# Layer 0's expert stage with one fixed stream of weights and rows read by number

## The chip, the cores and the metric

The kernel runs on one core of a Trainium2 chip. It computes a whole two-layer model in one launch. The metric is the device time of one launch in microseconds (us), as the median of several runs. The engines are named as in the profile: PE multiplies matrices (PEld is its load of the stationary operand), DVE and ACT work on vectors, POOL is GpSimd, SP issues most transfers.

## The reference, cut to what matters

Each of the two layers ends in a mixture of 16 experts. Every token takes its best group of four experts, and in it the best two:

```python
def hier_moe(h, wg, bg, we, be, w1, w3, w2):
    ...
    combine = jnp.sum(jax.nn.one_hot(eid, N_EXPERTS, dtype=F32) * wts[..., None], axis=1)
    out = jnp.zeros((T, D), F32)
    for e in range(N_EXPERTS):
        y = (jax.nn.silu(h @ w1[e]) * (h @ w3[e])) @ w2[e]
        out = out + combine[:, e:e + 1] * y
    return out.astype(h.dtype)
```

In layer 0, T is 512 (256 latent and 256 context tokens), D is 1024, and an expert is 512 wide. Its weights are 1024x512 twice and 512x1024, in 32 bits: 6.29 MB an expert. Behind the mixture, the tokens (`x`) get its output times a gate, and layer 1 begins with a norm and a projection.

## The kernel before, in words

The change lies in layer 0's expert stage, `experts` with `all0`. The router has put each expert's tokens into a list of at most 96 (`cap`). The 512 tokens stand as four tiles of 128 (`NT`), each split into two parts, `hhi` and `hlo`: PE multiplies in a form that keeps fewer bits, so a factor is taken as high part plus low part, and a product is three matmuls (high by high, high by low, low by high). `split` (line 220) makes the two parts: ACT copies the high one (`whi`, `XT`, `gT`), then DVE subtracts it (`wlo`).

**The lists.** Experts go in four groups of four, so one group's lists have 4 x 96 = 384 places (`N`). `lists(g)` writes a matrix of zeros and ones, `Pg`, which has a one where a token stands at a place: DVE writes all four tiles of group 0 (L609), and half of those of later groups, POOL the other half (L614). `gather(g, k)` multiplies a 128-column piece of the token tiles with `Pg`, in eight matmuls of 128x384 (`ga`), and splits the result into `XT`. Eight such pieces make a group's rows. `gather_next(e)` does two of the next group's eight beside each expert.

**An expert.** `start0` reads eight units of weights (512 KB each, a DMA that SP issues) into a ring of eight places (`slots`: four of them in the stage's own pool, four in another), splits each unit and does its six matmuls of 96x512 (`h`). Then SiLU on ACT, the product on DVE (`gg`, L652), four transposes on PE (`gT`), and in `finish0` four units of `w2`, again six matmuls each, into two banks `y`. ACT copies one half of `y` (L819), DVE the other (L820), and POOL stores the 96 rows to the table `yD` in device memory. `start0` is a generator: the loop over `e` begins expert e+1 before it finishes e. Apart from that order of the code and a few order tokens, a scheduler (Tile) places the instructions on the engines' queues.

**The combination.** Experts 0 to 13 leave their rows in `yD`. After expert 13's code, eight indirect reads on POOL bring each token's two rows into `rooms`. During expert 15, ACT scales one row (L790), DVE adds the other and multiplies with the gate `g2` (L791, L792), POOL adds the result to `x` (L793). The last two experts don't go through the table: their `y` is scaled and split by `weighted` (L763, L764), multiplied with transposed ones (`PT`) into `sc`, and added to `x` by `add_y` (L767, L768). Then layer 1's norm follows, `norm_T1` (L327 on): it loads the norm's weights and four modulation rows, makes `whi<-whi,xn` (L338), squares (L344), scales (L345, L352), transposes, and the first projection `pj` can start.

**Full lists.** A list that overflows is caught by `beyond` (L671 on): a loop on all engines, whose count `nexp` is read from memory. For the data here the count is zero, so the loop is only crossed. In layer 0 its code stands behind expert 12's, in layer 1 at the end.

Of the kernel before, what the change touches and what calls it, by code (L numbers as in the profile page):

```python
# [11 lines left out]
F32 = mybir.dt.float32  # L12
F32R = mybir.dt.float32r
# [8 lines left out]
P = 128  # L22
# [7 lines left out]
NCST = 1268  # L30
# [24 lines left out]
def host_consts():  # L55
# [16 lines left out]
    c[:, C_SMALL:C_SMALL + 16] = np.arange(16)  # L72
    c[:, C_SMALL + 16:C_SMALL + 32] = np.tril(np.ones((4, 4)), -1).ravel()
# [58 lines left out]
def tile_kernel(ctx: ExitStack, tc: tile.TileContext, I, out, stage=99, dbg=None):  # L132
# [293 lines left out]
    def moe(l, tiles, cap, ng, x1, pm, pn, hhi, hlo):  # L426
# [165 lines left out]
        def experts(pe, ysb, rest, spare=None):  # L592
# [5 lines left out]

            def lists(g):

                Pg = pe.tile([P, NT, N] if l == 0 else [P, NT, ng, 2, cap], F32R, tag="Pg", name="Pg")
                iota = cst[:, C_IOTA + 1:C_IOTA + 1 + cap]
                for a in range(NT):
                    if l == 1:
                        V.tensor_tensor(Pg[:, a], iota[:, None, None, :].to_broadcast([P, ng, 2, cap]),
                                        rk[:, a, g * ng:(g + 1) * ng, None, None].to_broadcast([P, ng, 2, cap]),
                                        op=ALU.is_equal)
                    elif g == 0 or a % 2:
                        V.tensor_tensor(Pg[:, a].rearrange("p (e c) -> p e c", e=ng),  # L609
                                        iota[:, None, :].to_broadcast([P, ng, cap]),  # L610
                                        rk[:, a, g * ng:(g + 1) * ng, None].to_broadcast([P, ng, cap]), op=ALU.is_equal)
                    else:
                        for e in range(ng):
                            G.tensor_scalar(Pg[:, a, e * cap:(e + 1) * cap], iota, rk[:, a, g * ng + e:g * ng + e + 1],  # L614
                                            None, op0=ALU.is_equal)
                XT = [pe.tile([P, 8, N], dt, tag=f"XT{i}", name="XT", bufs=2)
                      for i, dt in enumerate((F32R, F32R) if l == 0 else (F32,))]
                groups[g] = (Pg, XT)

            def gather(g, k):  # L620

                Pg, XT = groups[g]
                acc = ps("ga", "ga")
# [8 lines left out]

            def start0(e, es_, XT):

                hs = []
                for m in ("moe_w1", "moe_w3"):
                    acc = ps("h", "h")
                    hs.append(acc[0:cap, :])
                    for hh in range(4):
                        w = wload(I[m][l, e, hh * 256:(hh + 1) * 256, :], 2, 512)  # L640
                        whi, wlo = split_tiles()
                        split(w, whi, wlo)
                        for kk_ in range(2):
                            k = hh * 2 + kk_
                            mm(acc[0:cap, :], XT[0][:, k, es_], whi[:, kk_], start=(k == 0), stop=False)
                            mm(acc[0:cap, :], XT[0][:, k, es_], wlo[:, kk_], start=False, stop=False)
                            mm(acc[0:cap, :], XT[1][:, k, es_], whi[:, kk_], start=False, stop=(k == 7))
                        if hh < 3 or m == "moe_w1":
                            yield
                gg = pe.tile([P, 512], F32, tag="gg", name="gg", bufs=l + 1)  # L650
                act(gg[0:cap], hs[0], AF.Silu)
                V.tensor_tensor(gg[0:cap], gg[0:cap], hs[1], op=ALU.mult)  # L652
                yield gg

            def finish0(e, gg):
                acc = ps("gT", "gT")
                for f in range(4):
# [1139 lines left out]
```

## Time and profile before

| | us |
|---|---|
| median of 3 runs | 1466.31 (1465.74 to 1469.53) |
| the profiled execution, its own time | 1464.7 |
| its span in the trace | 1462.9 |
| PE busy over the span | 1282.3 (88%) |
| DVE busy | 810.3 (55%) |
| ACT busy | 601.8 (41%) |
| POOL busy | 239.9 (16%) |

The profile is of one execution. Its time is 1.6 us below the median. What lies around the span is 1.8 us. The shares of the whole span mix stages: the expert stage of layer 0, from about 535 to 913 us, is read from its own stretches below. "Granted clock" is the share of full speed that PE was given in a stretch; 1.00 is its upper level, 2.4 GHz.

### The profile page before, as it was taken

To read this page: it belongs to the slowest core of one execution; us is meant where nothing else is said; L and a number is where in the kernel's file an instruction comes from. 1 tells how busy PE (TensorE), PEld (TensorE's weight loads), DVE (VectorE), ACT (ScalarE), POOL (GpSimd) and SP (SyncE) were. 2 spreads that over 40 slices of the span, in tenths; PEclk is the share of its full clock that TensorE was granted. 3 is DMA by queue.
4 is the path that set the end of the run, shared out by engine and by line. 5 is a ranking of instruction groups with operands and counts; after the bars stand their busy time and mean duration, and the time that the engine had idled before them with its cause. 6 is when DMAs were issued, how large, how long until landed. Compare 5 with 4: busy or idle time off the path is not lost. (4 is left out here: it accounts for less than half of the span.)

```text
span 1462.9 us, 22162 instructions
## 1 busy us (share of the span) xinstructions
PE 1282.3 (88%) x8412; PEld 829.1 (57%) x8412; DVE 810.3 (55%) x1492; ACT 601.8 (41%) x1000; POOL 239.9 (16%) x245
## 2 busy tenths in 40 slices
PE   5999778888979968999999786789998799998975
PEld 1556556666646756777777553677665644433321
DVE  1336846777746665888888668963627520110003
ACT  2752422222224334777777564433637321211102
POOL 1005422424113203030110025420000100000000
PEclk9999889998999969999999998799998889999998
DMA  9687677766772544999999787562352579999654
GB/s 343 212 253 234 180 192 180 196 181 162 199 239 78 210 141 161 335 322 332 318 338 337 271 298 259 130 172 73 101 208 64 191 256 394 394 395 393 250 218 171
DMA packets 237859, 342.93 MB, mean 234 GB/s; under 512 B 95192, under 2 KB 125176, under 8 KB 237488
## 3 DMA queue, kind: packets, MB, share of 16 engines
q1 hardware_dynamic: 226240, 304.72, 62.6%
q0 software_dynamic: 8800, 28.42, 5.9%
q10 hardware_dynamic: 2704, 8.27, 1.6%
q8 instruction: 70, 1.15, 0.3%
q14 instruction: 45, 0.37, 0.1%
HBM read 320.57 MB, written 20.79 MB: 233 GB/s over the span
## 5 line engine op out<-in xcount | busy, mean ns | idle before, releaser
L220 DVE TENSOR_TENSOR wlo<-w,whi 128x1024 fp32r<-128x1024 f32 (+1 forms) x296 | 322.7, 1103 | 153.2 <-ACT whi L220 147.2
L220 ACT ACTIVATE whi<-w 128x1024 fp32r<-128x1024 f32 (+1 forms) x296 | 273.0, 932 | 236.2 <-DMA w<-in_ev_w_in_dram 69.5
L210 PE MATMUL h<-whi,XT 128*96 128x512 f32 x512 | 167.7, 401 | 12.2 <-issue 8.4
L210 PE MATMUL pj<-hh,whi 128*128 128x512 f32 x432 | 147.9, 424 | 0.3 <-ACT hh L220 0.3
L210 PE MATMUL h<-w,XT 128*64 128x512 f32 x512 | 138.5, 614 | 5.4 <-DMA w<-in_moe_w_dram 5.4
L210 PEld LDWEIGHTS h<-whi,XT 128*96 128x96 f32 x512 | 84.1, 164 | 50.5 <-issue 9.8
L210 PE MATMUL h<-wlo,XT 128*96 128x512 f32 x256 | 102.7, 401 | 6.0 <-DVE wlo L220 6.0
L210 PEld LDWEIGHTS pj<-hh,whi 128*128 128x128 f32 x432 | 82.1, 198 | 31.7 <-issue 9.8
L210 PE MATMUL pj<-hh,wlo 128*128 128x512 f32 x216 | 89.2, 415 | 3.3 <-DVE wlo L220 3.1
L210 PE MATMUL y<-whi,gT 128*96 128x512 f32 x256 | 87.4, 413 | 4.4 <-ACT gT L220 1.7
L210 PE MATMUL ada<-w,sT 128*32 128x512 f32 x384 | 69.6, 652 | 16.0 <-DMA w<-in_ada_w_dram 9.4
L210 PEld LDWEIGHTS h<-w,XT 128*64 128x64 f32 x512 | 36.6, 138 | 64.0 <-issue 56.9
L764 DVE SCALAR_TENSOR_TENSOR ylo<-y,sw,yhi 128x512 fp32r<-128x512 f32 x16 | 12.0, 751 | 100.9 <-ACT yhi L763 100.9
L210 PE MATMUL y<-w,gT 128*64 128x512 f32 x256 | 64.7, 614 | 1.5 <-ACT gT L697 1.5
L688 DVE TENSOR_TENSOR gg<-gg,h 64x512 f32<-64x512 f32 x16 | 11.1, 692 | 95.0 <-ACT gg L687 95.0
L210 PE MATMUL ga<-Pg,hh 128*128 128x384 f32 x256 | 58.5, 358 | 4.7 <-POOL Pg L614 3.5
L210 PEld LDWEIGHTS y<-whi,gT 128*96 128x96 f32 x256 | 41.8, 167 | 27.4 <-DVE gT L220 5.3
L210 PEld LDWEIGHTS h<-wlo,XT 128*96 128x96 f32 x256 | 42.2, 165 | 25.0 <-DVE wlo L220 8.8
L210 PE MATMUL y<-wlo,gT 128*96 128x512 f32 x128 | 51.9, 405 | 3.7 <-DVE wlo L220 3.7
L210 PEld LDWEIGHTS ga<-Pg,hh 128*128 128x128 f32 x256 | 47.6, 199 | 10.7 <-POOL Pg L614 3.9
L210 PEld LDWEIGHTS pj<-hh,wlo 128*128 128x128 f32 x216 | 42.8, 198 | 18.0 <-DVE wlo L220 5.9
L1769 POOL TENSOR_TENSOR x<-x,fg 128x512 f32<-128x512 f32 x2 | 2.8, 1378 | 283.8 <-ACT sq L1768 283.8
(534 smaller groups left out, 2309.6 us busy)
## 6 DMA issues: line engine op xcount, KB each, us to landing
w<-in_moe_w_dram SPq DMA_DIRECT2D x384, 512.0 KB, 6.5
w<-in_ada_w_dram SPq DMA_DIRECT2D x96, 512.0 KB, 5.2
w<-in_ev_w_in_dram SPq DMA_DIRECT2D x27, 512.0 KB, 5.8
w<-in_od_w_in_dram SPq DMA_DIRECT2D x24, 512.0 KB, 4.6
yD<-ysb POOLq DMA_DIRECT2D x14, 384.0 KB, 6.3
sD<-wad SPq DMA_DIRECT2D x16, 256.0 KB, 3.1
w<-in_ev_w_out_dram SPq DMA_DIRECT2D x8, 512.0 KB, 4.4
w<-in_od_w_out_dram SPq DMA_DIRECT2D x8, 512.0 KB, 4.2
```

The source lines that it names most:

```text
L210: inst = nc.tensor.matmul(*args, **kw)
L220: for inst in (act(hi, src, AF.Copy), V.tensor_tensor(lo, src, hi.bitcast(F32), op=ALU.subtract)):
L688: V.tensor_tensor(gg[64:128], gg[64:128], acc[64:128], op=ALU.mult)
L764: V.scalar_tensor_tensor(lo, y, w, hi.bitcast(F32), op0=ALU.mult, op1=ALU.subtract))
L1769: (V if h else G).tensor_tensor(xt_[:, hs], xt_[:, hs], fg[:, hs], op=ALU.mult)
```

## The change

1. The lists of group 0 are gathered as before. The row order on PE is written out: gathers of four pieces, a unit of weights, two pieces, a unit, two pieces.
2. For groups 1 to 3 there are no gathers. `one_hot0` writes `Pg` (all on DVE), `ids` multiplies it with the tokens' numbers (a new constant, `C_TOK`) in 16 matmuls of one column, `fetch(e)` reads the expert's 96 rows of the normed tokens from device memory (`hD`) with one indirect DMA on POOL, `turn_rows` transposes them (8 transposes an expert) and splits them into `XE`.
3. Weights go as one `stream` of units; `weights(e, u)` has units split up to three ahead of their use. Eight more places of 512 KB are added to the ring, and taken out again behind expert 10.
4. PE, ACT and DVE follow the order in which the code is written, by order tokens ("line" for PE, "moe" for ACT and DVE).
5. Both halves of `y` are copied by ACT.
6. The rooms' sums go between expert 15's later units, as before in effect; reading them is issued at the end of expert 13's step.
7. `beyond` stands behind the last `add_y`.

The core of the diff:

```diff
+            def ids(g, Pg, put):
+                acc = ps("sw", "ga")
+                idt[g] = pe.tile([P, ng], I32, tag="idt", name="idt", bufs=2)
+                for i in range(ng):
+                    for a in range(NT):
+                        mm(acc[r, i:i + 1], Pg[:, a, i * cap:(i + 1) * cap], cst[:, C_TOK + a:C_TOK + a + 1],
+                           start=(a == 0), stop=(a == NT - 1))
+                put(V.tensor_copy(idt[g][r], acc[r, 0:ng]))
+            def fetch(e):
+                if ng <= e < 16:
+                    g, i = divmod(e, ng)
+                    xe[e] = pe.tile([P, D], F32, tag="xe", name="xe", bufs=2)
+                    nc.gpsimd.indirect_dma_start(
+                        out=xe[e][0:cap, :], out_offset=None, in_=hD,
+                        in_offset=bass.IndirectOffsetOnAxis(ap=idt[g][0:cap, i:i + 1], axis=0))
+            def turn_rows(e, h):
...
+                acc = ps("xt", ("ga", "ps")[h])
+                for k in range(4):
+                    flip(acc[:, k * cap:(k + 1) * cap], xe[e][0:cap, (4 * h + k) * 128:(4 * h + k + 1) * 128],
+                         ident[0:cap, 0:cap])
+                split(acc[:, 0:4 * cap].rearrange("p (k c) -> p k c", k=4), XTe[e][0][:, 4 * h:4 * h + 4],
+                      XTe[e][1][:, 4 * h:4 * h + 4])
...
+                slots.extend([(pP, t, 1, h) for t in ("kT", "y", "kkn") for h in range(2)] +
+                             [(cp, "x3", 1, h) for h in range(2)])
...
+                stream = [(0, u) for u in range(8)]
+                for e in range(15):
+                    stream += [(e + 1, 0), (e + 1, 1)] + [(e, u) for u in range(8, 12)] + [(e + 1, u) for u in range(2, 8)]
+                stream += [(15, u) for u in range(8, 12)]
...
+                def weights(e, u):
+                    ready(place[e, u] + 3)
+                    return there.pop((e, u))
...
+                in_line[0] = True
+                token[0] = "moe"
+                put = lambda inst: inorder(inst, "moe")
+                for k in range(4):
+                    gather(0, k, ("ga", "gT")[k % 2])
+                hidden(0, 0)
...
                     if e < 14:
                         o = ysb[:, e % 2, :]
-                        act(o[r, 0:512], y[0], AF.Copy)
-                        V.tensor_copy(o[r, 512:1024], y[1])
+                        for h in range(2):
+                            put(act(o[r, h * 512:(h + 1) * 512], y[h][r], AF.Copy))
                         nc.gpsimd.dma_start(yD[e * cap:(e + 1) * cap, :], o[r, :])
...
-                    gather_next(e)
-                    if e == 12:
...
-                        beyond(rooms)
...
+                    turn_rows(e + 2, 0)
+                    hidden(e + 1, 3)
+                    turn_rows(e + 2, 1)
+                    if j == 0 and g + 1 < NG:
+                        one = one_hot0((g + 1) * ng, ng, F32, put)
...
+                    for u in range(4, 8):
+                        hidden(e + 1, u)
+                        if u == 4 and j == 0 and g + 1 < NG:
+                            ids(g + 1, one, put)
...
                         add_y(t, hs_, acc, ysb[:, a % 2, hs_])
+                beyond(rooms)
+                warm(AF.Sqrt, rooms[0])
```

Line numbers of the changed kernel are 2 higher in front of the expert stage (L212 for L210, L222 for L220).

PE at the start of the stage. `ga` are the gathers, `h` the products with the first units of weights. Before:

```order
L210 MATMUL ga<-Pg,hh 128x384 x8
L210 MATMUL h<-whi,XT 96x512
L210 MATMUL h<-wlo,XT 96x512
L210 MATMUL ga<-Pg,hh 128x384 x8
L210 MATMUL h<-whi,XT 96x512 x2
L210 MATMUL h<-wlo,XT 96x512
L210 MATMUL ga<-Pg,hh 128x384 x8
```

And after:

```order
L212 MATMUL ga<-Pg,hh 128x384 x32
L212 MATMUL h<-whi,XT 96x512
L212 MATMUL h<-wlo,XT 96x512
L212 MATMUL h<-whi,XT 96x512 x2
L212 MATMUL h<-wlo,XT 96x512
L212 MATMUL h<-whi,XT 96x512
L212 MATMUL ga<-Pg,hh 128x384 x16
```

The gathers stand in blocks of 32 and 16, and a unit's six products are whole between them.

PE inside an expert, before, where gathers (`ga`) for the next group stand among the transposes and products:

```order
L210 MATMUL h<-whi,XT 96x512
L210 MATMUL ga<-Pg,hh 128x384 x2
L215 MATMUL gT<-cst,gg 128x96 x4
L210 MATMUL ga<-Pg,hh 128x384 x5
L210 MATMUL y_6423<-whi,gT 96x512
```

After, in the same place of a later expert, `xt` are the transposes of the rows read by number:

```order
L212 MATMUL y<-whi,gT 96x512 x2
L212 MATMUL h<-whi,XE 96x512
L212 MATMUL h<-wlo,XE 96x512
L212 MATMUL h<-whi,XE 96x512 x2
L212 MATMUL h<-wlo,XE 96x512
L212 MATMUL h<-whi,XE 96x512
L217 MATMUL xt<-cst,xe 128x96 x4
L212 MATMUL h<-whi,XE 96x512
```

Sixteen gathers an expert are gone, and eight transposes have come, in two blocks of four around a unit.

DVE where the stage ends, before; L338 and L345 to L347 are layer 1's norm:

```order
L764 SCALAR_TENSOR_TENSOR spare<-y_8862,sw,spare 96x512
L767 TENSOR_TENSOR ysb<-sc,g2t 128x512 x2
L338 SCALAR_TENSOR_TENSOR whi<-whi,xn 128x1024 x2
L768 TENSOR_TENSOR x_4758<-ysb,x_4758 128x512 x2
L767 TENSOR_TENSOR ysb<-sc,g2t 128x512 x2
L345 TENSOR_TENSOR xn<-x_4758,whi 128x512
L346 TENSOR_TENSOR st<-st 128x1
L768 TENSOR_TENSOR x_4758<-ysb,x_4758 128x512
```

And after, the last sums with what follows them; the rows from `nexp` on are the loop's:

```order
L764 TENSOR_TENSOR ysb<-sc,g2t 128x512 x2
L765 TENSOR_TENSOR x_4757<-ysb,x_4757 128x512 x2
L222 TENSOR_TENSOR wlo<-w,whi 128x512
L678 TENSOR_LOAD nexp
L679 COMPARE_AND_BRANCH
L679 UNCONDITIONAL_BRANCH x2
L1892 BRANCH_PREFETCH_HINT
```

The other twelve sums stand ahead of these in the same pairs. All sixteen are now ahead of the loop's branch, and every instruction of layer 1's norm behind it.

## Rows read from the trace of the kernel before

**Rows 1.** Stretches of 20 us, then one of layer 1: busy us by engine, granted clock, DMA

```profile
core 0: us, PE busy (x) PEld busy (x) DVE busy (x) ACT busy (x) POOL busy (x), PEclk, DMA share, GB/s
...
740.00:760.00 20.00, 20.00 (x92) 14.52 (x92) 16.86 (x17) 14.71 (x17) 0.55 (x1) 1.00 0.97 348
...
860.00:880.00 20.00, 16.83 (x74) 11.12 (x73) 16.35 (x16) 14.92 (x17) 11.02 (x9) 1.00 1.00 378
...
1210.00:1250.00 40.00, 40.00 (x193) 18.27 (x194) 3.80 (x6) 6.96 (x15) 0.00 (x0) 1.00 1.04 394
```

**Rows 2.** Timeline, start and length: ACT first reads y of experts 0, 11, 14, 15

```profile
581.49 0.58 ACT L819 ACTIVATE ysb<-y 96x512 f32<-96x512 f32 x1
...
805.42 0.58 ACT L819 ACTIVATE ysb<-y 96x512 f32<-96x512 f32 x1
...
877.69 1.24 ACT L763 ACTIVATE spare<-y,sw 96x512 fp32r<-96x512 f32 x2
...
911.83 1.38 ACT L763 ACTIVATE spare<-y,sw 96x512 fp32r<-96x512 f32 x2 [3.19 <-PE y L210]
```

**Rows 3.** Timeline of PE, from expert 11's last gather to expert 12's transposes

```profile
805.41 1.49 PEld L210 LDWEIGHTS ga<-Pg,hh 128*128 128x128 f32 x8
...
817.88 1.58 PEld L210 LDWEIGHTS sw<-comb,Pg 128*96 128x96 f32 x16
...
819.41 0.53 PE L215 MATMUL gT<-cst,gg 96*128 96x96 f32 x4
```

**Rows 4.** Lines by form, 580 to 820 us: busy, mean ns | idle before it

```profile
L220 DVE TENSOR_TENSOR wlo<-w,whi 128x1024 fp32r<-128x1024 f32 x143 | 173.8, 1224 | 30.3 <-ACT whi L220 28.8
...
L220 DVE TENSOR_TENSOR XT<-ga,XT 128x384 fp32r<-128x384 f32 x23 | 12.7, 553 | 5.7 <-ACT XT L220 5.7
...
L652 DVE TENSOR_TENSOR gg<-gg,h 96x512 f32<-96x512 f32 x12 | 8.1, 676 | 0.0
...
L609 DVE TENSOR_TENSOR Pg<-cst,rk 128x384 fp32r<-128x384 f32 x4 | 2.3, 576 | 0.0
```

**Rows 5.** Timeline of PE at the start: gathers of list 0, wait for list 1

```profile
540.65 2.77 PE L210 MATMUL ga<-Pg,hh 128*128 128x384 f32 x8
...
571.53 1.14 PEld L210 LDWEIGHTS ga<-Pg,hh 128*128 128x128 f32 x4 [3.95 <-POOL Pg L614]
```

**Rows 6.** DMA issues, 530 to 940 us: count, KB, median us to landing

```profile
yD<-ysb POOLq DMA_DIRECT2D x14, 384.0 KB, 6.3
...
wlo<-adaD POOLq DMA_DIRECT2D x2, 512.0 KB, 4.2
...
room<-yD,idx POOLq DMA_INDIRECT x8, 8.9
```

**Rows 7.** Lines by form, 876 to 913 us

```profile
L220 DVE TENSOR_TENSOR wlo<-w,whi 128x1024 fp32r<-128x1024 f32 x12 | 18.9, 1605 | 2.5 <-ACT whi L220 2.5
...
L793 POOL TENSOR_TENSOR x<-room,x 128x1024 f32<-128x1024 f32 x4 | 13.5, 3364 | 9.7 <-DVE room L792 9.7
```

**Rows 8.** Timeline at the full lists' loop, layer 0, then layer 1

```profile
831.59 1.23 DVE L220 TENSOR_TENSOR wlo<-w,whi 128x1024 fp32r<-128x1024 f32 x1 [0.15 <-ACT whi L220]
...
838.89 0.74 PE L210 MATMUL h<-whi,XT 128*96 128x512 f32 x1 [8.42 <-issue]
...
1403.02 0.69 DVE L688 TENSOR_TENSOR gg<-gg,h 64x512 f32<-64x512 f32 x1 [7.22 <-ACT gg L687]
...
1404.61 1.30 SPq L701 DMA_DIRECT2D w<-in_moe_w_dram  x3
```

**Rows 9.** Timeline from layer 0's last expert to layer 1's first projection

```profile
912.54 1.45 DVE L764 SCALAR_TENSOR_TENSOR spare<-y,sw,spare 96x512 fp32r<-96x512 f32 x2 [2.65 <-ACT spare L763]
...
918.91 1.29 DVE L768 TENSOR_TENSOR x<-ysb,x 128x512 f32<-128x512 f32 x2
...
919.63 0.63 ACT L344 ACTIVATE xn<-x 128x512 f32<-128x512 f32 x1 [3.87 <-DVE x L768]
...
935.05 0.79 PE L210 MATMUL pj<-rT,whi 128*128 128x256 f32 x2
```

More of the change, by code (lines that the diff above doesn't have):

```diff
@@ L631, in gather @@
                     act(XT[0][:, k], acc[:, 0:N], AF.Copy)
[L633 to L653, printed above, removed]
@@ L705, in finish1 @@
                 return y
-            start, finish = ((start0, finish0), (start1, finish1))[l]
             def beyond(room):
@@ L775, in all0, with without @@
                 nc.gpsimd.dma_start(yD[Z:Z + P, :], zt)
-                rooms = []
                 order = [(2, 2), (3, 3), (0, 0), (1, 1)]
                 r = slice(0, cap)
-                steps = begin(0)
+                base = list(slots)
+                slots.extend([(pP, t, 1, h) for t in ("kT", "y", "kkn") for h in range(2)] +
+                             [(cp, "x3", 1, h) for h in range(2)])
+                turn[0] = 0
+                def without(tags):
+                    n = len(slots)
+                    slots[:] = [s_ for s_ in (slots[(turn[0] + i) % n] for i in range(n)) if s_[1] not in tags]
+                    turn[0] = 0
@@ new lines, in weights, with hidden @@
+                def weights(e, u):
+                    ready(place[e, u] + 3)
+                    return there.pop((e, u))
+                hs = {}
+                def hidden(e, u):
+                    X, es_ = (XTe[e], r) if e in XTe else (groups[0][1], slice(e * cap, (e + 1) * cap))
+                    whi, wlo = weights(e, u)
+                    if u % 4 == 0:
+                        hs[e, u // 4] = ps("h", "h")[r, :]
+                    acc = hs[e, u // 4]
+                    for i in range(2):
+                        k = u % 4 * 2 + i
+                        mm(acc, X[0][:, k, es_], whi[:, i], start=(k == 0), stop=False)
+                        mm(acc, X[0][:, k, es_], wlo[:, i], start=False, stop=False)
+                        mm(acc, X[1][:, k, es_], whi[:, i], start=False, stop=(k == 7))
@@ new lines, in all0 @@
+                    for f in range(4):
+                        flip(acc[:, f * cap:(f + 1) * cap], gg[r, f * 128:(f + 1) * 128], ident[r, 0:cap])
+                    gT = [pe.tile([P, 4, cap], F32R, tag=f"gT{i}", name="gT", bufs=2) for i in range(2)]
+                    split(acc[:, 0:4 * cap].rearrange("p (f c) -> p f c", f=4), *gT)
+                    if e < 15:
+                        hidden(e + 1, 1)
+                    y = [ps("y", "y") for _ in range(2)]
+                    for f in range(4):
+                        whi, wlo = weights(e, 8 + f)
+                        for i, (gh, w) in enumerate(((gT[0], whi), (gT[0], wlo), (gT[1], whi))):
+                            for h in range(2):
+                                mm(y[h][r], gh[:, f, :], w[:, h], start=(f == 0 and i == 0), stop=(f == 3 and i == 2))
```

206 lines of the change are left out of this document (117 added, 89 removed).

## The prediction

> **What bounds the kernel now.** I read the 20 us stretches first, then the dated rows of one engine, then the lines by form for the price of a row. In a steady stretch of layer 0's experts PE is busy 20.00 of 20 us at granted clock 1.00, DVE 16.86, ACT 14.71, and the transfers run at 348 GB/s with a share of 0.97 [rows 1]. So PE's own work ends last, with transfers close behind. That the transfers can do more is seen twice in the same group: 378 GB/s between 860 and 880 us, 394 in layer 1.
>
> The stage is dated by the moment at which ACT first reads an expert's `y` [rows 2]. Expert 0 is at 581.49, expert 11 at 805.42: 223.93 / 11 = 20.36 us per expert. Expert 14 is at 877.69, so experts 0 to 14 take 296.2, and expert 15 takes 34.1 more (911.83). The 14 periods at 20.36 would be 285.0; the other 11 us are around the loop and expert 13's extra work.
>
> What is PE's 20.36 made of? Between the end of the gathers at 805.41 + 1.49 = 806.90 and the next foreign row at 817.88 [rows 3] stand 48 products of 512 columns with no gap: 10.98 / 48 = 0.229 each. An expert has 72: 16.47 us. Its four transposes take 0.53 (0.132 each). Sixteen gathers at 1.49 / 8 = 0.186 take 2.98. Sum 19.98, so 0.38 of a period is waiting.
>
> **The change, part by part.** The sum is made against the profiled execution, 1464.7 us, which is 1.6 below the median of the runs.
>
> *Gathers out, rows by number in.* PE loses 2.98 per expert and gains eight transposes, 8 x 0.132 = 1.06, for experts 4 to 15. From the first `y` of expert 0 to that of expert 14 PE now has 14 x (16.47 + 0.53) = 238.0; transposes of 12 experts, 12.7; the numbers of three groups, 16 one-column products each, for which the 16 loads of `sw` in 1.58 us [rows 3] are the like: 4.7; the ones of experts 14 and 15, eight transposes and as many small products, 2.6 at most. Sum 258.0. That is the floor.
>
> *Waiting on top.* DVE per expert: 12 `wlo` at 1.224, `gg` 0.676, the low part of `gT` and two of `XE`, 128x384 each like `XT`, at 0.553, together 17.0; and in each group four `Pg` at 0.576 [rows 4], 0.6 per expert. Copying half of `y` goes to ACT, which had 5.3 us of 20 free. So DVE has 17.6 us to do in a PE period of 18.06, while its order is now fixed and weights may be split only three units ahead. I take 0.7 us of waiting per expert, about twice the 0.38 of now, and 1 us for each of the three bursts of `Pg` (2.3 us on DVE in one piece, partly under split units): 12.8. So experts 0 to 14 take 258.0 + 12.8 = 270.8 where they took 296.2: **25.4 won**. Ends: no waiting beyond the present rate wins 33 (14 x 0.38 = 5.3); at the present period of 20.36 only the loop's detour is won, some 11. The plain expert is then 18.75 us.
>
> *Places and transfers.* Per expert 12 x 524 KB, 393 KB of rows read and 393 KB stored to `yD`: 7.08 MB, in 18.75 us 378 GB/s, where it is 6.68 MB in 20.36 now, 328 GB/s. The 14 periods need 99.1 MB. Eight more places let 4.2 MB be there before expert 0 is through, since nothing but free places holds them back; the remaining 94.9 MB in 270.8 us is 350 GB/s, as in the steady row [rows 1]. I therefore cost transfers at nothing, with little to spare: if the lead is lost, the rival below takes over. One row read on POOL is of the size of a room's read, 8.9 us to landing [rows 6], and is asked for over one period ahead of its transposes: nothing.
>
> *The start.* PE now does 8 x 4 gathers at once, without waiting for units in between, and no longer stands 3.95 us for lists that POOL writes [rows 5]. Behind that wait it ran at half clock, as at 540.65, where eight gathers took 2.77 instead of 1.49. The two are worth at most 3.95 + some 5. Against it, the first products wait for the last piece's split and for unit 0 behind it. I take 5 of 0 to 9.
>
> *Expert 15.* The four sums of rooms on ACT, DVE and POOL stay; DVE's `wlo` took 1.605 instead of 1.224 there, and POOL's adds 3.364 each [rows 7]. PE loses nothing but waits. Without the transfers queued behind the loop I take 1.4 won, 8 either way.
>
> *The loop to the end.* At layer 0's loop DVE's last row ended at 832.82 and PE went on at 838.89, 6.1 us; at layer 1's, with no transfers in flight, SP went on 0.9 us behind DVE's end [rows 8]. At its new place little is in flight: I take 2.5 of 0.9 to 6.1. Dearer is what it parts. Now, the sums begin at 912.54, the norm's squares at 919.63 among them, and the projection starts at 935.05 [rows 9]: 22.5 us. After it, all 16 additions and multiplications at 0.645 (1.29 for two) must end first: 10.3, and 2.1 in front of them for `weighted` and the first `sc`: 12.4. Then the loop, 2.5. Then the norm from its start: 919.63 to 935.05 is 15.4 as it stands, with additions in between that fall away; but the load of the norm's weights (512 KB, like `wlo<-adaD`, 4.2 us [rows 6]) stands behind the loop now, and products wait for it. I take 18 of 15 to 22. Sum 32.9 for 22.5: **10.4 lost**, 6 to 18.
>
> *Sum.* 25.4 + 5 + 1.4 - 10.4 = 21.4 won: 1443.3 for the profiled execution, 1445 for the median.
>
> **The rivals.**
>
> *Transfers bound.* If the lead isn't made or doesn't last, the 99.1 MB go at the steady row's 348 GB/s: 284.8 us for 270.8, and 14 less is won: 1459. For it speak the share of 0.97; against it 378 and 394 GB/s in other rows. The Trainium skill ("DMA: Bandwidth & Descriptors", Specifications) gives a core about 358 GB/s from device memory, and says in its Bandwidth section that this side binds for loads. By that figure the same 99.1 MB would be 277 us and the time about 1451, an estimate from that page; the rows of 378 and 394 GB/s disagree with the limit.
>
> *The fixed order starves PE (slower).* The place is DVE with ACT in front of it: 17.6 us of work per expert, in written order, where a late `XE` or `gT` also holds the `wlo` behind it. Today DVE is busy 16.86 of 20, 0.84. If a fixed order lets it no closer, an expert takes 17.6 / 0.84 = 20.9 us; 14 x (20.9 - 18.75) = 30 more: 1475. It decides from 14 x 1.5 = 21.4 on, that is above 20.3 us per expert. Against it: 48 products without a gap while ACT and DVE split beside them [rows 3].
>
> *No waiting and a cheap end.* Waiting stays at 0.38 (gain 33 for 25.4), the start gives 7, the end costs 7: 1432.
>
> *It doesn't do what it says.* Were row reads late by one landing, 8.9 us, at each of three groups' first expert, 27 would go: 1472. The numbers are ready five units before, so this is little.
>
> **How the numbers follow.** Forecast 0.60, transfers 0.13, fixed order 0.12, cheap end 0.12, late reads 0.03. The forecast's own range is 1433 to 1457 (start 4, waiting 8, expert 15 8, end 6, not all at once). From the cheap end's 1432 less a little to the transfers' 1459 and some way toward the fixed order: 1430 to 1464. A measurement tells some 0.3%, 4.4 us, from no change. Faster: the forecast, the cheap end and three quarters of the transfers' case, 0.82. Same: the rest of that and the milder fixed order, 0.06. Slower 0.12.
>
> **What would show it.** Right: first reads of `y` 18.5 to 19 us apart at expert 5 and after, no `ga` rows past 560 us, `xt` rows of 0.5 in their place; PE still the full engine; DVE near 0.93 busy; the first `y` near 576; projection `pj` some 33 us behind the first `weighted`. Wrong: PE waiting for `w` (through ACT's `whi`) with a DMA share of 1.00, which is the transfers; PE waiting for `wlo` with DVE full, the fixed order; for `xe`, late reads. A period of 20 or more makes the prediction fall.

## The result and the profile after

The changed kernel takes 1446.94 us (median of 4, 1445.39 to 1453.49), the kernel before 1466.03 beside it. The ratio is 0.9877, with an interval of 0.984 to 0.9915: 19 us faster, where 21 were forecast (1445). The profiled execution's span is 1445.2 us, 17.7 less than before.

Those 17.7 are not all the change's. The router's last product, `rk`, stands ahead of everything that was edited. In the profile of before it lies at 534.54:

```profile
534.54 0.38 PE L210 MATMUL rk<-sel,tri 128*128 128x80 bf16 x5 [3.15 <-DVE sel L522]
```

In the profile after it is 3.9 us earlier (columns: start, length, engine, line, operation):

```profile
530.67 0.38 PE L212 MATMUL rk<-sel,tri 128*128 128x80 bf16 x5 [3.15 <-DVE sel L524]
```

So the stage is measured from `rk` to the first projection of layer 1, `pj`: before 935.05 [rows 9] - 534.54 = 400.5, after 917.12 - 530.67 = 386.5 us, 14.1 won. A second profile of the changed kernel gave 387.7. The four pieces are dated by ACT's first reads of `y`, as in [rows 2] (timeline of ACT, experts 0, 1, 3, 4, 5, 13, 14, 15):

```profile
571.36 1.05 ACT L870 ACTIVATE ysb<-y 96x512 f32<-96x512 f32 x2
...
596.43 1.06 ACT L870 ACTIVATE ysb<-y 96x512 f32<-96x512 f32 x2
...
632.22 1.06 ACT L870 ACTIVATE ysb<-y 96x512 f32<-96x512 f32 x2
...
650.43 1.06 ACT L870 ACTIVATE ysb<-y 96x512 f32<-96x512 f32 x2
...
674.75 1.06 ACT L870 ACTIVATE ysb<-y 96x512 f32<-96x512 f32 x2
...
826.50 1.06 ACT L870 ACTIVATE ysb<-y 96x512 f32<-96x512 f32 x2
...
849.80 1.24 ACT L760 ACTIVATE spare<-y,sw 96x512 fp32r<-96x512 f32 x2
...
884.07 1.26 ACT L760 ACTIVATE spare<-y,sw 96x512 fp32r<-96x512 f32 x2 [3.69 <-PE y L212]
```

| piece | before | after | won | forecast |
|---|---|---|---|---|
| `rk` to expert 0's `y` | 46.95 | 40.69 | 6.3 | 5 |
| expert 0's to 14's `y` | 296.20 | 278.44 | 17.8 | 25.4 |
| 14's to 15's `y` | 34.14 | 34.27 | -0.1 | 1.4 |
| 15's `y` to `pj` | 23.22 | 33.05 | -9.8 | -10.4 |

A period is the time from one expert's first read of `y` to the next one's. A plain expert's is 18.2 us (650.43 - 632.22), that of the one in which a group's list is made 24.3 (674.75 - 650.43), the first of these 25.1 (596.43 - 571.36). In 20 us stretches (busy us by engine, clock, DMA), a plain one, one with a list, and expert 15:

```profile
core 0: us, PE busy (x) PEld busy (x) DVE busy (x) ACT busy (x) POOL busy (x), PEclk, DMA share, GB/s
...
620.00:640.00 20.00, 19.76 (x94) 13.61 (x93) 18.10 (x18) 16.41 (x21) 2.26 (x2) 1.00 1.04 377
640.00:660.00 20.00, 18.53 (x104) 13.38 (x103) 17.16 (x20) 12.91 (x17) 1.23 (x2) 0.98 1.04 382
...
860.00:880.00 20.00, 6.30 (x17) 4.00 (x18) 16.54 (x11) 2.53 (x4) 9.44 (x4) 0.51 0.19 61
```

These answer to [rows 1]. PE, now under 20 by its few waits, still ends last in the plain stretch; DVE is at 18.10, 0.91; transfers at 377 to 382 GB/s and a share of 1.04, above the steady 348 of before. In the last stretch PE works for 6.30 of 20 us.

What is in the 24.3? The timeline behind expert 4's `y`, PE and DVE:

```profile
653.18 0.62 PE L212 MATMUL h<-whi,XE 128*96 128x512 f32 x2
...
654.46 1.96 DVE L606 TENSOR_TENSOR Pg<-cst,rk 128x384 f32<-128x384 f32 x4
...
655.15 3.68 PE L212 MATMUL sw<-cst,Pg 128*96 128x1 f32 x32 [0.89 <-DVE Pg L606]
...
658.70 0.45 PE L212 MATMUL h<-whi,XE 128*96 128x512 f32 x1
...
659.32 1.05 PE L212 MATMUL h<-whi,XE 128*96 128x512 f32 x2
```

and the clock around it, in stretches of 2 us:

```profile
660.00:662.00 2.00, 2.00 (x6) 1.25 (x6) 0.18 (x1) 0.74 (x1) 1.00 (x1) 0.50 0.84 278
...
664.00:666.00 2.00, 2.00 (x9) 1.13 (x7) 1.62 (x2) 1.77 (x3) 0.00 (x0) 1.00 0.81 244
```

PE waits 0.89 for the ones, then does the numbers in 3.55 us (655.15 to 658.70): 32 rows of one column for the 16 products in the code. When the products of weights come back, the clock is at 0.50, its lower level: two products in a row end in 1.05 us instead of 0.62. Full clock is back before 664: some 3.5 us at half clock, which cost about 1.7. 0.9 + 3.55 + 1.7 make the 6.1 by which 24.3 exceeds 18.2.

Expert 15, on DVE, POOL and PE:

```profile
854.66 1.28 DVE L908 SCALAR_TENSOR_TENSOR room<-room,wk 128x1024 f32<-128x1024 f32 x1
...
859.84 0.58 ACT L848 ACTIVATE gg<-h 96x512 f32<-96x512 f32 x1
...
863.00 3.25 POOL L910 TENSOR_TENSOR x<-room,x 128x1024 f32<-128x1024 f32 x1 [2.42 <-DVE room L909]
...
863.97 3.36 DVE L908 SCALAR_TENSOR_TENSOR room<-room,wk 128x1024 f32<-128x1024 f32 x1
...
874.18 0.68 DVE L849 TENSOR_TENSOR gg<-gg,h 96x512 f32<-96x512 f32 x1
...
874.92 0.90 PE L217 MATMUL gT<-cst,gg 96*128 96x96 f32 x4 [13.22 <-DVE gg L849]
```

ACT had the SiLU ready at 860.4. DVE's product with it ran at 874.18, behind four sums of rooms, so PE waited 13.22 us. The first such sum took 1.28 us, the three that ran while POOL added to `x` took 3.36 to 3.41. And the end, which answers to [rows 9]:

```profile
884.78 1.41 DVE L761 SCALAR_TENSOR_TENSOR spare<-y,sw,spare 96x512 fp32r<-96x512 f32 x2 [3.15 <-ACT spare L760]
...
894.58 1.28 DVE L765 TENSOR_TENSOR x<-ysb,x 128x512 f32<-128x512 f32 x2
...
896.83 1.28 ACT L231 ACT_TABLE_LOAD   x1 [10.47 <-DVEq L679]
...
898.36 0.34 ACTq L334 DMA_DIRECT2D xn<-in_norm_g_dram  x1
...
902.54 2.36 DVE L340 SCALAR_TENSOR_TENSOR whi<-whi,xn 128x1024 f32<-128x1024 f32 x2 [2.08 <-DMA xn<-in_norm_g_dram]
...
917.12 1.01 PE L212 MATMUL pj<-rT,whi 128*128 128x256 f32 x3
```

The sums end at 895.9, the loop is crossed by 896.8 (DVEq L679 is its branch), the norm's weights are asked for at 898.36 and used at 902.54, and the projection starts at 917.12: 32.3 us from the weighted copies, forecast 32.9.

### The profile page after: what moved, and what is told of

It is laid out like the page before. It is cut to its first block, busy times and chain, and to the rows that moved or that the text cites. A ratio compares the mean times of both kernels' runs of the same rounds, so it can differ in the third digit from the quotient of the medians.

```text
span 1445.2 us, 22098 instructions
## 1 busy us (share of the span) xinstructions
PE 1264.2 (87%) x8412; PEld 813.8 (56%) x8412; DVE 810.4 (56%) x1491; ACT 604.2 (42%) x1014; POOL 222.7 (15%) x233
## 5 line engine op out<-in xcount | busy, mean ns | idle before, releaser
L222 DVE TENSOR_TENSOR wlo<-w,whi 128x1024 fp32r<-128x1024 f32 (+1 forms) x296 | 323.8, 1108 | 139.9 <-ACT whi L222 132.7
L222 ACT ACTIVATE whi<-w 128x1024 fp32r<-128x1024 f32 (+1 forms) x296 | 272.4, 933 | 208.6 <-DMA w<-in_ev_w_in_dram 74.9
L212 PE MATMUL pj<-hh,whi 128*128 128x512 f32 x432 | 148.0, 424 | 0.3 <-ACT hh L222 0.3
L212 PE MATMUL h<-w,XT 128*64 128x512 f32 x512 | 138.2, 613 | 5.3 <-DMA w<-in_moe_w_dram 5.3
L212 PE MATMUL h<-whi,XE 128*96 128x512 f32 x384 | 133.5, 408 | 0.0
L212 PEld LDWEIGHTS pj<-hh,whi 128*128 128x128 f32 x432 | 82.5, 199 | 31.9 <-issue 9.8
L212 PE MATMUL pj<-hh,wlo 128*128 128x512 f32 x216 | 88.9, 413 | 2.9 <-DVE wlo L222 2.7
L212 PE MATMUL ada<-w,sT 128*32 128x512 f32 x384 | 70.4, 660 | 19.3 <-DMA w<-in_ada_w_dram 12.2
L212 PE MATMUL h<-wlo,XE 128*96 128x512 f32 x192 | 78.2, 407 | 1.7 <-DVE wlo L222 1.7
L212 PEld LDWEIGHTS h<-whi,XE 128*96 128x96 f32 x384 | 63.8, 166 | 24.9 <-issue 0.5
L212 PE MATMUL y<-whi,gT 128*96 128x512 f32 x256 | 73.4, 398 | 0.0
L212 PEld LDWEIGHTS h<-w,XT 128*64 128x64 f32 x512 | 36.6, 138 | 63.9 <-issue 56.7
L212 PE MATMUL y<-w,gT 128*64 128x512 f32 x256 | 64.4, 614 | 1.5 <-ACT gT L661 1.5
L652 DVE TENSOR_TENSOR gg<-gg,h 64x512 f32<-64x512 f32 x16 | 11.1, 691 | 95.0 <-ACT gg L651 87.8
L212 PEld LDWEIGHTS pj<-hh,wlo 128*128 128x128 f32 x216 | 42.7, 197 | 17.6 <-DVE wlo L222 5.5
L212 PEld LDWEIGHTS y<-whi,gT 128*96 128x96 f32 x256 | 42.1, 165 | 18.7 <-ACT gT L222 0.4
L1867 POOL TENSOR_TENSOR x<-x,fg 128x512 f32<-128x512 f32 x2 | 2.7, 1374 | 284.8 <-ACT sq L1866 284.8
L871 POOL DMA_DIRECT2D yD<-ysb x14 | 7.4, 531 | 248.9 <-ACT ysb L870 248.9
L212 PE MATMUL h<-whi,XT 128*96 128x512 f32 x128 | 44.2, 412 | 1.5 <-ACT whi L222 1.5
L651 ACT ACTIVATE gg<-h 64x512 f32<-64x512 f32 x16 | 9.4, 588 | 77.9 <-PE h L212 77.9
L212 PEld LDWEIGHTS h<-wlo,XE 128*96 128x96 f32 x192 | 32.0, 166 | 15.7 <-DVE wlo L222 4.9
```

The costliest lines, as they stand in the source:

```text
L212: inst = nc.tensor.matmul(*args, **kw)
L222: for inst in (act(hi, src, AF.Copy), V.tensor_tensor(lo, src, hi.bitcast(F32), op=ALU.subtract)):
L651: act(gg[64:128], acc[0:64], AF.Silu)
L652: V.tensor_tensor(gg[64:128], gg[64:128], acc[64:128], op=ALU.mult)
L871: nc.gpsimd.dma_start(yD[e * cap:(e + 1) * cap, :], o[r, :])
L1867: (V if h else G).tensor_tensor(xt_[:, hs], xt_[:, hs], fg[:, hs], op=ALU.mult)
```

## The experiments

The changed kernel was run once more beside e10 and e11:

> The changed kernel once more, unedited, beside the two others of this group. Expected near 1447, with plain experts at 18.2 us in every execution; if the half clock behind the one-column products is a matter of chance, its experts with lists differ from the 24.3 us of the first profile by up to 3 us.

Its experts with lists took 24.3 again (the first 25.1 again), and 1452.6 us, later than the expected 1447, stand beside a kernel before of 1468.4 on that chip: its ratio, 0.9906, lies within the interval of the first.

Each run is read by the same pieces, from its profile; the median and the ratio to the kernel before on the same chip stand beside them. Layer 1's stretch from the first projection to its output products, which no edit touches but in its first rows, takes from 192 to 201 us in these profiles, with stretches at lower clock in some. A few us of a median are that, which is why `rk` to `pj` is the better measure of the edits.

| run | rk to y0 | y0 to y14 | to y15 | to pj | rk to pj | median | ratio (interval) |
|---|---|---|---|---|---|---|---|
| before | 46.95 | 296.2 | 34.1 | 23.2 | 400.5 | 1466.03 | |
| after | 40.7 | 278.4 | 34.3 | 33.1 | 386.5 | 1446.94 | 0.9877 (0.984 to 0.9915) |
| e9 after again | 40.7 | 278.5 | 34.3 | 34.3 | 387.7 | 1452.6 | 0.9906 (0.9885 to 0.9927) |
| e1 spread | 40.6 | 281.8 | 34.3 | 33.9 | 390.5 | 1454.57 | 0.9922 (0.9897 to 0.9946) |
| e2 late sums | 39.7 | 278.0 | 17.6 | 46.4 | 381.7 | 1445.31 | 0.9845 (0.9806 to 0.9884) |
| e3 eight places | 39.1 | 282.9 | 37.3 | 34.6 | 393.9 | 1455.16 | 0.9934 (0.9896 to 0.9972) |
| e4 gathered | 40.5 | 284.3 | 35.9 | 33.5 | 394.2 | 1453.08 | 0.9915 (0.9883 to 0.9946) |
| e5 wide numbers | 41.0 | 265.0 | 33.0 | 33.8 | 372.9 | 1435.45 | 0.9821 (0.9767 to 0.9875) |
| e6 no loop, after | 39.1 | 282.4 | 34.2 | 25.7 | 381.5 | 1440.97 | 0.9827 (0.9796 to 0.9858) |
| e7 no loop, before | 46.8 | 286.8 | 33.7 | 23.0 | 390.4 | 1462.29 | 0.9972 (0.994 to 1.0003) |
| e8 best | 40.8 | 265.1 | 20.7 | 28.9 | 355.7 | 1419.09 | 0.966 (0.9613 to 0.9706) |
| e10 wide, eight places | 41.0 | 268.9 | 38.7 | 34.3 | 382.9 | 1439.61 | 0.9789 (0.9731 to 0.9846) |
| e11 loop in the middle | 40.6 | 284.2 | 33.2 | 25.8 | 383.8 | 1445.22 | 0.9847 (0.9805 to 0.9889) |
| e12 best, loop in the middle | 40.8 | 274.8 | 18.5 | 26.3 | 360.4 | 1423.44 | 0.97 (0.9654 to 0.9746) |

### What an expert with a list costs: e1, e5

```diff
-                        if u == 4 and j == 0 and g + 1 < NG:
-                            ids(g + 1, one, put)
+                        if j == 0 and g + 1 < NG:
+                            ids(g + 1, one, put, u - 4)
```

> The changed kernel with the numbers of a group's lists spread: one expert's four one-column products behind each of the four units 4 to 7, instead of all sixteen behind unit 4. Theory (the block of one-column products takes 3.5 us and PE then works at half clock, which costs 2.6 more): an expert with a list takes some 21.7 us instead of 24.3, no stretch of half clock behind it, 3 x 2.6 = 8 us less in all, about 1439. Rival (the 6.1 us are the products and the wait for the ones on DVE, the clock costs nothing): list experts stay near 24, the time within 2 us of the changed kernel's 1447.

Both theories missed. Experts with lists took 26.2, 28.6 and 23.9 us, 78.7 in all, where the unedited block took 73.7 (25.1, 24.3, 24.4). The clock in 2 us stretches around the second of them:

```profile
664.00:666.00 2.00, 2.00 (x6) 1.39 (x5) 0.86 (x1) 0.00 (x0) 0.00 (x0) 0.50 1.03 410
...
672.00:674.00 2.00, 2.00 (x7) 1.23 (x6) 1.23 (x2) 0.00 (x0) 2.00 (x1) 0.50 0.03 8
...
676.00:678.00 2.00, 2.00 (x11) 1.38 (x10) 1.55 (x2) 1.23 (x3) 0.00 (x0) 1.00 0.76 279
```

Spread out, the small products keep PE at the lower clock from about 662 to 675 us, longer than one block of them did. So the clock is a good part of what they cost, and thinning the small products out doesn't spare it. That it costs more when thinned isn't shown: in the profiles of e3 and e6 the three experts with the unedited block take 79.3 us. The next run takes them away:

```diff
-                for i in range(ng):
-                    for a in range(NT):
-                        mm(acc[r, i:i + 1], Pg[:, a, i * cap:(i + 1) * cap], cst[:, C_TOK + a:C_TOK + a + 1], ...)
+                for a in range(NT):
+                    mm(acc[r, 0:N], tokb[:, a], Pg[:, a], start=(a == 0), stop=(a == NT - 1))
+                put(V.tensor_tensor(own[r], acc[r, 0:N].rearrange("p (e c) -> p e c", e=ng),
+                                    ident[r, None, 0:cap].to_broadcast([cap, ng, cap]), op=ALU.mult))
+                put(V.tensor_reduce(num[r], own[r], axis=AX, op=ALU.add))
```

> The changed kernel with the numbers of a group's lists made by four products of 384 columns (a constant tile that holds the tokens' numbers in every column, times the ones) and a pick of the diagonal on DVE, in place of sixteen products of one column. Theory (the one-column products and the half clock behind them are what an expert with a list costs over 18.2): no half clock, the products take 0.75 us, list experts 19.5 to 20.5 instead of 24.3, 12 to 14 us won, about 1434. Rival (the wait for the ones on DVE lowers the clock and costs the time): list experts stay at 22 or more, at most 5 us won.

```profile
646.20 1.95 DVE L606 TENSOR_TENSOR Pg<-cst,rk 128x384 fp32r<-128x384 f32 x4
...
646.89 1.73 PE L212 MATMUL sw<-Pg,tokb 128*96 128x384 f32 x4 [0.90 <-DVE Pg L606]
...
648.46 0.40 PE L212 MATMUL h<-whi,XE 128*96 128x512 f32 x1
...
648.93 0.63 PE L212 MATMUL h<-whi,XE 128*96 128x512 f32 x2
```

The theory holds: four products, paced by the ones that DVE writes beside them, 1.6 us in all, and the products behind them at 0.40 and 0.63, full clock. Experts with lists take 20.06, 20.92 and 20.93 us. Experts 0 to 14 take 265.0 where the changed kernel takes 278.4: 13.4 won, of 12 to 14 expected. Of these, 1.6 stand at expert 14 (21.7 for 23.3), whose own small products this edit doesn't touch. They are followed by clock 0.50 in the changed kernel (834 to 836 us) and by 1.00 in e2 (832 to 836), which leaves them alone too and also takes 21.7: this part is chance. The wait for the ones, 0.90, is as long as before the edit, so the rival (that the wait lowers the clock) falls. The edit changes the products' width and their form (f32 to fp32r) together, so it shows what the sixteen products cost, not which of the two makes it. Its four executions lie from 1427.69 to 1452.05, 24 us apart, like the 21 of e8, e10 and e12; those of the other edited kernels lie 3 to 18 apart. Why isn't known. The profile is of the fastest, but those of e8 and e12 show the same 20.1 and 20.9.

### Rows by number, the order, the places: e4, e3, e10

```diff
-                    turn_rows(e + 2, 0)
                     hidden(e + 1, 3)
-                    turn_rows(e + 2, 1)
...
-                        if u == 4 and j == 0 and g + 1 < NG:
-                            ids(g + 1, one, put)
+                        if more:
+                            k = more.pop(0)
+                            gather(g + 1, k, ("ga", "ps")[k % 2])
```

> The changed kernel's stream of units and written order, but with the gathers of before for groups 1 to 3 in place of reading rows by number (three pieces an expert in the first three experts of a group), and with eight places, since the token tiles that the gathers read lie where the additional places would be. Theory (reading by number saves 23 us of PE work but pays 18 for the numbers, and the order saves the rest of the waits): experts 0 to 14 take 284 us where the changed kernel takes 278, about 1453. Rival (the gain is the rows by number, the order gives nothing): experts 0 to 14 take 290 or more, 1460 or later.

Experts 0 to 14 took 284.3, expected 284. The `y` of experts 4 and 5 in its timeline, then the twelve periods from expert 0's to 12's `y`, in this run and in the kernel before (columns as in [rows 1]):

```profile
650.69 1.06 ACT L866 ACTIVATE ysb<-y 96x512 f32<-96x512 f32 x2
...
672.70 1.06 ACT L866 ACTIVATE ysb<-y 96x512 f32<-96x512 f32 x2
...
568.74:814.65 245.91, 240.57 (x1106) 175.71 (x1105) 204.93 (x204) 178.95 (x218) 6.09 (x12) 1.00 0.91 327
...
581.49:825.91 244.42, 242.73 (x1114) 174.96 (x1113) 206.86 (x208) 177.59 (x204) 27.14 (x28) 1.00 0.94 329
```

An expert with three pieces of gathers takes 22.0 us (672.70 - 650.69), one without any 17.6. The number is the theory's, but the mechanism isn't: the twelve periods take 245.9 us, where the kernel before takes 244.4, and PE stands idle for 5.3 us of them (245.91 - 240.57), where it was 1.7. So the written order and the units split ahead saved no waits inside the experts. This run wins 6.3 of `rk` to `pj` over before: 6.4 at the start and 13.4 at experts 13 and 14, where the loop stood, less 1.5 in the twelve periods, 1.7 in expert 15 and 10.3 at the end. The next run keeps rows by number and takes the places back:

```diff
-                slots.extend([(pP, t, 1, h) for t in ("kT", "y", "kkn") for h in range(2)] +
-                             [(cp, "x3", 1, h) for h in range(2)])
```

> The changed kernel without the eight additional places for weights (eight in all, as before). Theory (transfers run at 377 to 389 GB/s in the plain stretches, all that they can, and the lead of 4.2 MB lets PE go on): PE waits for weights, plain experts go from 18.2 to 18.7 us or more, 6 to 10 us are lost, about 1454. Rival (PE's work alone sets the period, the places do nothing): plain experts stay at 18.2, time within 2 us of 1447.

It is no faster than the gathers: 393.9 against 394.2. The 23 us that PE saves on gathers are eaten by three lists at 25 to 27 us, by weights late in expert 15 (37.3 us) and once by a plain expert of 18.7. But two of its lists took 27.1, like two in e6 with all places and unlike the 24.3 of the changed kernel: that difference (5.6 us) can't be put down to the places. With wide numbers the clock was expected to leave the comparison alone (the same edit of the places, on the kernel of e5):

> The kernel with wide numbers, without the eight additional places. Here no half clock hides what the places do. Theory (transfers at 380 GB/s just feed PE, the lead covers the rest): PE waits for weights, experts 0 to 14 take 4 to 8 us more than the 265 us with sixteen places, about 1441. Rival (the places do nothing): experts 0 to 14 within 1 us of 265, the time within 3 us of 1435.

```profile
847.00 1.24 ACT L763 ACTIVATE spare<-y,sw 96x512 fp32r<-96x512 f32 x2
...
885.67 1.26 ACT L763 ACTIVATE spare<-y,sw 96x512 fp32r<-96x512 f32 x2 [3.17 <-PE y L212]
```

Experts 0 to 14 take 3.9 us more than with sixteen places (268.9 against 265.0), the first two with lists 21.6 and 22.3 instead of 20.1 and 20.9, several plain ones 18.5 instead of 18.2, and expert 15 takes 38.7 (847.00 to 885.67) instead of 33.0, with ACT waiting 4.24 us for a unit of weights there: 9.5 in all. But the clock disturbs this pair too: in the expert of 22.3 us it falls to 0.51 (660 to 662 us), where it stays at 1.00 in e5, so up to 1.4 of the 9.5 can't be put down to the places. The medians differ by 4, within their spread. The places hang on the rows by number: six of the eight lie where the gathers would still read the token tiles.

### The loop: e6, e7, e11

```diff
-                beyond(rooms)
                 warm(AF.Sqrt, rooms[0])
```

> The changed kernel with layer 0's loop for full lists left out. Theory (the loop parts the sums from layer 1's norm): from the first weighted copy of expert 15 to the first projection 22 to 24 us instead of 32.3, some 9 us won, about 1438. Rival (the norm is late in any case, the loop costs its crossing alone): at most 3 us won.

```profile
882.66 1.41 DVE L761 SCALAR_TENSOR_TENSOR spare<-y,sw,spare 96x512 fp32r<-96x512 f32 x2 [3.13 <-ACT spare L760]
...
888.81 0.63 ACT L346 ACTIVATE xn<-x 128x512 f32<-128x512 f32 x1 [4.57 <-DVE x L765]
...
907.63 0.79 PE L212 MATMUL pj<-rT,whi 128*128 128x256 f32 x2
```

Norm and sums interleave again, the squares start at 888.81, and from the weighted copies to `pj` it is 25.0 us, against 32.3: 7.4 won there. And in the kernel before:

```diff
-                        beyond(rooms)
                     if e == 13:
```

> The kernel before with layer 0's loop for full lists left out. Theory (the loop behind expert 12 stops all engines): expert 13 comes 20.4 to 21.5 us behind expert 12 instead of 32.1, some 11 us won, about 1455. Rival (the transposed ones of the last experts cost it, as the changed kernel's 23.3 us of expert 14 suggest): 26 us or more, at most 6 won.

Expert 13 comes 22.25 us behind expert 12 instead of 32.1, 9.9 won, and `rk` to `pj` is 10.1 less. The median shows only 4 of it: its profile has a stretch of layer 1, 1380 to 1420 us, at clock 0.83, which is at 0.96 in the profile of before. Its interval reaches 1.0003, so the time alone doesn't tell it from no change. So the loop cost 10 where it was and 7 where it is. What if only the loop goes back?

> The changed kernel with the loop for full lists put back behind expert 12's step; the rest of the change stays. Theory (the loop costs some 10 us there and 7 at the end): expert 13 comes 27 to 30 us behind expert 12, the end from the weighted copies to the projection shrinks from 32 to 25, in sum 2 to 5 us slower than the changed kernel, about 1450. Rival (with PE close to full all the time the loop's stop costs no more than its crossing, as at the end): 3 us or more faster, 1443 or less.

```diff
+                    if e == 12:
+                        rooms = []
...
+                        beyond(rooms)
...
-                beyond(rooms)
                 warm(AF.Sqrt, rooms[0])
```

```profile
819.54 1.22 DVE L222 TENSOR_TENSOR wlo<-w,whi 128x1024 fp32r<-128x1024 f32 x1
...
823.54 0.74 PE L212 MATMUL h<-whi,XE 128*96 128x512 f32 x1 [5.48 <-issue]
```

PE stops for 5.48 us there and starts at half clock, expert 13's period is 25.5 instead of 18.2: 7.3 lost, less than the 10 of the kernel before. The end takes 25.8 instead of 33.1 or 34.3, and expert 15 takes 33.2 instead of 34.3. In sum `rk` to `pj` is 383.8 against 386.5 and 387.7. Of that, 1.6 is expert 14 at 21.7 instead of 23.3, and this isn't the loop's place: with the loop at the end e1, e2 and e3 take 21.7 too. What is left is 1 to 2 us, in one profile, and the intervals of the times overlap (0.9805 to 0.9889 here, 0.984 to 0.9915 for the changed kernel). The expected loss didn't come, and the rival's gain of 3 us isn't shown either (1445.22, where it said 1443 or less). Moving the loop to the end won nothing that can be told.

### Expert 15 and the end: e2, e8, e12

```diff
-                        if e == 14:
-                            a, t = order[u - 4]
...
+                        if e == 15:
+                            a, t = order[f]
```

> The changed kernel with the four sums of rooms moved on ACT and DVE from between expert 15's last four units of hidden products to behind its SiLU product, beside its four second-matrix units. Theory (PE stands 13 us in expert 15 since DVE's product of the SiLU is queued behind the sums): the wait for that product falls from 13 to under 2 us; weighted then waits for DVE's sums, so 6 to 9 us are won, about 1439. Rival (DVE has to do the sums before the end in any case, so the wait only moves to the weighted copies): within 2 us of 1447.

```profile
856.77 0.55 PE L217 MATMUL gT<-cst,gg 96*128 96x96 f32 x4 [0.64 <-DVE gg L849]
...
863.56 3.39 DVE L869 SCALAR_TENSOR_TENSOR room<-room,wk 128x1024 f32<-128x1024 f32 x1
...
878.28 1.40 DVE L761 SCALAR_TENSOR_TENSOR spare<-y,sw,spare 96x512 fp32r<-96x512 f32 x2
...
879.08 8.52 PE L212 MATMUL sc<-spare 96*128 96x512 f32 x23 [12.59 <-DVE spare L761]
```

PE gets its SiLU product at once (a wait of 0.64), expert 15 takes 17.6 us. But DVE is then busy with the rooms until 878.28, and PE waits 12.59 for the weighted copies. Of the 16.7 us won in expert 15, the end gives 12.2 to 13.4 back (46.4 against 34.3 and 33.1): 3 to 5 stay, and the median is 1.6 below the changed kernel's. That is the rival's case. The lever is DVE's work itself, part of which is lost to GpSimd: the first of these sums took 1.28 us, the next, beside POOL's addition, 3.39. The Trainium skill ("SBUF — State Buffer", the section on its two separate sides) says that VectorE and GpSimd share a pair of ports as an exclusive lock, so that the loser waits for the other's whole instruction; the two durations agree with that: POOL's addition runs from 863.18 to 865.87, and the sum that starts at 863.56 ends at 866.95, about one sum's length later. So the best version takes POOL out:

```diff
+                        mm(acc, ident, rooms[2 * order.index((a, t))][:, h * 512:h * 512 + 512], start=True, stop=False)
...
-                            put(V.tensor_tensor(y0, y0, g2[t], op=ALU.mult))
-                            G.tensor_tensor(token_tile(x1, t), y0, token_tile(x1, t), op=ALU.add)
...
+                nextg["ngb"] = ring0.tile([P, D], F32, tag="w", name="ngb", bufs=NRING)
...
-                (V if h else G).tensor_tensor(n[:, hs], token_tile(x, t)[:, hs], sc[i][:, hs], op=ALU.mult)
+                V.tensor_tensor(n[:, hs], token_tile(x, t)[:, hs], sc[i][:, hs], op=ALU.mult)
```

> The changed kernel with four edits: the wide numbers of the run before; the rooms' sums behind expert 15's SiLU product as in the run with late sums, but without their product with the gate and without GpSimd: PE adds the rooms to the products of the transposed ones (one more 32-bit product of 512 columns for each half), and the gate multiplies the sum; layer 1's norm weights loaded ahead of the loop into a place of the ring; all of that norm's products on DVE, none on GpSimd. Theory: 13 us from the numbers, 6 as in the late sums and some 10 more since DVE has 5 us of rooms' work instead of 25, 3 to 5 from the norm's weights: about 1417. Rival (DVE is not what holds the end, PE's 32-bit products take the won time): 1430 or more.

```profile
860.50 3.67 DVE L874 SCALAR_TENSOR_TENSOR room<-room,wk 128x1024 f32<-128x1024 f32 x3
...
863.23 1.26 ACT L763 ACTIVATE spare<-y,sw 96x512 fp32r<-96x512 f32 x2 [0.79 <-PE y L212]
...
882.20 0.63 ACT L346 ACTIVATE xn<-x 128x512 f32<-128x512 f32 x1
...
887.05 1.97 PE L217 MATMUL nT<-cst,xn 128*128 128x128 f32 x8 [9.28 <-DVE xn L354]
...
892.17 0.80 PE L212 MATMUL pj<-rT,whi 128*128 128x256 f32 x2 [0.69 <-ACT rT L222]
```

Three sums of rooms end in 3.67 us, expert 15 takes 20.7, PE adds the rooms, the norm starts at 882.20 without waiting for its weights, and `pj` comes 28.9 us behind expert 15's `y`. The stage is 355.7 us, the median 1419.09 (1409.15 to 1429.78): 3.4% below the kernel before, and as expected (1417). Of the 30.8 us that the stage wins over the changed kernel, the experts up to 14 bring 13.3, as in e5, expert 15 brings 13.5 and the end 4.1; the three edits behind the numbers ran together, so what each is worth isn't shown. With the loop in the middle:

> The kernel with the four edits (wide numbers, rooms summed by PE, the norm's weights early, the norm's products on DVE), and the loop for full lists put back behind expert 12's step. Theory (the loop costs 7 us behind expert 12 and more at the end, where it keeps the norm from starting beside the last sums): from the router's last product to the first projection 3 to 8 us less than the 358.6 of the kernel with the loop at the end, the median about 1414. Rival (with the norm's weights loaded early the end is already short, and the loop's stop behind expert 12 is a loss): 361 us or more, 1422 or later.

(The 358.6 in this expectation was read off a later row; the first `pj` of e8 is at 892.17, so 355.7.) 360.4 us is close to the rival, which said 361 or more. The end shrinks by 2.6 only, since the weights are early, and expert 15 by 2.2; the experts up to 14 take 9.6 more with the loop's stop among them, of which 1.4 is expert 14, as in the changed kernel. In these two profiles the loop is better at the end, by 4.7 us; the medians, 1423.44 and 1419.09, don't tell them apart, since their ranges overlap almost whole.

## Why the prediction was right, and where its steps failed

**The number was right; the stage won less than was forecast.** Forecast were 21.4 won in the profile and 1445; measured are 14.1 in the stage, 17.7 with the luck ahead of it, and a median of 1446.94. That the time came within 2 us is in part luck: 19.1 us lie between the medians, 5 more than the stage won, and what lies ahead of `rk` took from 526 to 537 us in these profiles without any edit to it. The 14.1 are 6.3 at the start, 7.5 in the twelve periods from expert 0 to 12 (244.4 to 236.9) and 10.3 at experts 13 and 14 (51.8 to 41.5), where the loop stood, less 0.1 in expert 15 and 9.8 at the end. So nearly all that is left is the start and the rows read by number.

**The start** was right: 6.3 for 5. The gathers run in blocks with no wait for POOL, PE waits 1.5 us for the first split, 0.8 for its low part and hardly elsewhere.

**Waiting on top** was too high for a plain expert and far too low for one with a list. The floor of 18.06 came out right by two errors that cancel: the expert without transposes takes 17.6 where the sum had 17.0, and eight transposes add 0.6 where it had 1.06. Above it the waiting is 0.14 (18.20), not 0.7: a DVE at 0.91 starved nobody. So the rival of the fixed order, with its 20.9 us per expert, fell in the first profile, and so did the late reads: in the twelve periods PE waits 2.7 us for `gg` and 2.4 for `Pg`, and never for `xe`.

**The failed step is the numbers of three groups.** The text priced the 16 products of a group at 1.58 us, after 16 rows of `sw` [rows 3]. In the trace a 32-bit product of one column makes two rows; those 16 rows were eight products. The block takes 3.55, and behind it come 1.7 at half clock, for which the sum had nothing. With the 0.9 wait (forecast 1) a list costs 6.1, the first one 7.5, not 2.6: 12.0 more for the three. Expert 14, whose transposed ones go with the same small products, costs 5.1 more than a plain one where the sum had 2.6 at most. The plain experts give 6.9 back. Together that is 7.6, and turns 25.4 into 17.8. e5 shows it by taking the lists' products away: 13.4 come back, 11.8 of them in the lists. How much half clock follows the same block differs from one execution to the next.

**Expert 15** was forecast at a small gain, with an error of 8 either way, from the same four sums as before. The sums are the same, but the written order put them ahead of the SiLU product, and 13 us of waiting in one piece took the place of the waiting of before, 12 us in seven pieces of 0.9 to 3.5. The step named the risk on DVE and POOL, not its place.

**Transfers at nothing** was right, and as near the edge as it was said to be: 377 to 382 GB/s in plain stretches. The time alone doesn't decide against the rival of the transfers: experts 0 to 14 took 278.4 us, between the forecast's 270.8 and the rival's 284.8. e5 does, which moves the same units and rows in 265.0 us (368 GB/s on average). The Trainium skill's figure of some 358 GB/s for a core ("DMA: Bandwidth & Descriptors", Specifications), by which these bytes would have taken 277 us, an estimate from that page, is passed for the whole of the plain stretches; its Bandwidth section gives that figure for two cores that stream at once, and here one core works. The lead is needed, as e10 shows: without the places some 8 us are lost in its profile, most of them in expert 15.

**The end** was right to 0.6 us: 32.3 for 32.9, with the sums at 11.1 (forecast 12.4), the crossing at 1.0 (2.5) and the norm at 20.3 (18), in which DVE waits 2.1 for the norm's weights. What the text did not see is that the move wins nothing as a whole. It counted the 10 us saved in the middle and the 10 lost at the end in different terms, and never set them side by side; e11 does, and the two places come out within 1 to 2 us of each other.

Not tried: the changed kernel's parts with the start of before, so the 6.3 us of the start are read from the traces alone; and the written order without the stream of units and the places.

## What to carry to other kernels

Price a small product by rows of the trace, not by lines of code, and look at the clock behind a block of them: what follows pays as well. When an order is written out by hand, look for the one result that another engine waits for, and put it ahead of work that nobody waits for yet; if that work is needed right after, as in e2, the wait only moves, and the work itself has to shrink, as in e8. Before moving a barrier, write what it costs in both places next to each other, in the changed kernel: here 10 became 7.

## What was not expected of the hardware

- A 32-bit product of one column shows as two rows of 0.11 us each; 16 of them in a block take 3.55 us and leave PE at its lower clock for some 3.5 us after them. Four groups of four, with a unit of wide products between, keep it there for 13 us.
- The same block was followed by more or less half clock in different executions: experts with lists took 24.3, 25.5 or 27.1 us (the first of the three 25.1). The wide form took 20.1 in the first and 20.9 in the others in every profile with sixteen places; in e10, with eight, one took 22.3 with the clock at 0.51 for a stretch of 2 us.
- A sum on DVE of 128x1024 takes 1.28 us alone and 3.36 to 3.41 when it starts while GpSimd adds a tile of the same size.
- Transfers of 512 KB ran at 377 and 382 GB/s for stretches of 20 us beside a PE that was busy for 18.5 to 19.8 of them.
